# Low parts of two weight chunks per step by ScalarE and an accumulating DMA, in the MLPs of a two-layer hybrid decoder trunk

## The chip, the core and the metric

One NeuronCore of a Trainium2 chip runs the whole program. The metric is the device time of one execution in microseconds (us). Three runs of the kernel before gave 2110.32, 2111.22 and 2113.54 us; the median is 2111.22 us.

## The reference, cut to what matters

Everything is float32: 256 tokens, model width 2048, two layers. Each layer is a mixer and a squared-ReLU MLP with sandwich RMSNorm, and the MLPs are what the change touches:

```python
def sq_relu_mlp(u, w_up, w_down):
    return jnp.square(jax.nn.relu(u @ w_up)) @ w_down

for i in range(DEPTH):                       # DEPTH = 2
    u = rmsnorm(h, mix_pre_g[i])
    m = short_conv_mixer(...) if i == 0 else stick_breaking_mixer(...)
    h = h + rmsnorm(m, mix_post_g[i])
    u = rmsnorm(h, mlp_pre_g[i])
    h = h + rmsnorm(sq_relu_mlp(u, mlp_w_up[i], mlp_w_down[i]), mlp_post_g[i])
```

`w_up` is 2048 x 8192 and `w_down` 8192 x 2048 in each layer.

## The kernel before

**Two parts of every number.** TensorE multiplies in fp32r. Each weight is split into a high part, its fp32r rounding, and a low part, the weight minus the high part. A product is then three matmuls: high by high, high by low, low by high.

**Chunks.** All weights come in one stream of chunks of 128 x 1024 floats (512 KB). `load_one` (L148) issues a chunk's load on SyncE's queue (L157) into one of 5 `raw` buffers. `high_parts` (L167) writes the high part into one of 7 `hi` tiles on ScalarE (L173), and `low_part` writes the low part into one of 7 `lo` tiles on VectorE, as `raw - hi` (L184). A raw buffer is free for a later load when its last reader has finished. The next chunk's load is issued in stream order: SyncE waits at the first load whose buffer is not free, and all later loads wait behind it. The program splits chunks up to four ahead of their use (`chunk`, L239), but a hi or lo tile can be written only when TensorE has read what it held seven tiles earlier.

**An MLP.** Each MLP first computes one eighth of the hidden layer alone (`lead_up`), then runs eight steps `e` = 0 to 7. Steps 0 to 6 have 32 chunks in two halves of 16. A half alternates four times: two chunks of `w_up` for one tile of the next eighth (`whole_up`: 16 high matmuls, L1013, then 16 low ones, L1020), then two chunks of `w_down` for the present eighth (L1120 to L1122). So chunks 0, 1, 4, 5, 8, 9, 12 and 13 of a step belong to `w_up` in the first half; 2, 3, 6, 7 and so on are `w_down`. Most `w_down` pairs take Strassen-Winograd's seven products: `split_seven` makes four differences of the two raw chunks on VectorE (L210) and splits them in four pieces a, b, t, u (L218 on ScalarE, L184 on VectorE), which take four hi and four lo tiles for two chunks.

**What else VectorE and ScalarE do there.** When the up tile is done, ScalarE copies half of its bank out (`half`, L1026), VectorE adds the other half (`s`, L966), ScalarE takes ReLU and square (L967, L968), and both split the result (`hid`). All up tiles of the steps use one PSUM bank, so the next up tile cannot begin before L966 has read the last one.

**GpSimd.** It computes nothing here. Its queue issues accumulating DMAs (L1030, 128 x 512 floats, 256 KB, `mg<-more`) that add the extra products of the seven into the results, nine in each step; they are issued in the second half of a step.

**What sets the order.** TensorE's order is the program's; VectorE's and ScalarE's order in the MLP steps is set by the scheduler when the kernel is built, and so is the choice of the free buffer that a tile takes.

Of the kernel before, what the change touches and what calls it, by code (L numbers as in the profile page):

```python
# [9 lines left out]
F32 = mybir.dt.float32  # L10
F32R = mybir.dt.float32r
AF = mybir.ActivationFunctionType
ALU = mybir.AluOpType
# [33 lines left out]
STEPS = 8  # L47
# [48 lines left out]
def trunk(ctx, tc, x, xT, vecs, rows, ws, out):  # L96
    nc = tc.nc
# [45 lines left out]
    raw, parts, early = {}, {}, {}  # L143
    last_load = [None]
    count = {"loaded": 0, "split": 0, "limit": 1 << 30, "apart": False}
    lows = []
    sevens = {}

    def load_one():
        i = count["loaded"]  # L150
        if i >= len(stream):
            return
        w, c = stream[i]
        t = wpool.tile([P, CW], F32, tag="raw", name=f"raw{i}")
        n = HALF if i < FIRST else CW
        for a in range(0, CW, n):
            last_load[0] = nc.sync.dma_start(t[:, a : a + n], w.ap[c, :, a : a + n])  # L157
        raw[i] = t
        count["loaded"] += 1

    def pieces_of(i):
        w, c = stream[i]
        gains = w.gains(c) if w.gains else [None] * (4 if i < FIRST else 1)
        n = CW // len(gains)
        return [(slice(j * n, (j + 1) * n), gain) for j, gain in enumerate(gains)]

    def high_parts(i):  # L167
        while count["loaded"] <= i:
            load_one()
        hi = wsplit.tile([P, CW], F32R, tag="hi", name=f"whi{i}")  # L170
        lo = wsplit.tile([P, CW], F32R, tag="lo", name=f"wlo{i}")
        for j, (at, gain) in enumerate(pieces_of(i)):
            rounded = nc.scalar.activation(  # L173
                hi[:, at], raw[i][:, at], AF.Copy, scale=1.0 if gain is None else gain
            )
            if j < 2:
                early[i] = rounded
            if not count["apart"]:
                low_part(hi, lo, raw[i], at, gain)
        parts[i] = hi, lo  # L180

    def low_part(hi, lo, t, at, gain):
        if gain is None:
            nc.vector.tensor_tensor(lo[:, at], t[:, at], hi[:, at].bitcast(F32), op=ALU.subtract)  # L184
        else:
            nc.vector.scalar_tensor_tensor(  # L186
                lo[:, at], t[:, at], gain, hi[:, at].bitcast(F32), op0=ALU.mult, op1=ALU.subtract
            )
# [37 lines left out]
    def split_one():  # L226
        i = count["split"]
        if i in sevens:
            split_seven(i)
            return  # L230
        high_parts(i)
        count["split"] += 1
        if count["apart"]:
            lows.append(i)
        else:
            raw.pop(i)
            load_one()
# [138 lines left out]
    h = [None] * NB  # L376
# [310 lines left out]
    W = {"in": Weights(ws["in"]), "out": Weights(ws["out"])}  # L687
# [251 lines left out]
    def mlp(pool, i, before, after):  # L939
# [3 lines left out]
        scale = [None] * NB  # L943
# [89 lines left out]
        def lead_up(to):  # L1033
            first = W["mlp", i, 0].base
            place = {kn: m for m, kn in enumerate(UP_FIRST)}
            lead = list(range(LEAD_UP))
            alone = [(k, n) for k in range(ALONE) for n in lead]
            for b in range(NB):
                for k, n in sorted(alone, key=lambda kn: (kn[0] // 4, kn[1] // 3 if kn[0] < 4 else 0)):
                    high(first, place[k, n], k, n, n + 2, b)  # L1040
            for k, n in alone:
                low(first, place[k, n], k, n)
            for k in range(ALONE, KD):
                for n in lead:
                    high(first, place[k, n], k, n, n + 2)
                for n in lead:
                    low(first, place[k, n], k, n)
                    if k == KD - 1:
                        finish(to, n)
            for n in range(LEAD_UP, NF):  # L1050
                whole_up(to, n, first + 2 * n, (n + 2) % 8)
# [114 lines left out]
        for e in range(STEPS):  # L1166
            for h in range(2):
                for m in SEVEN[e][h]:
                    n = 16 * h + 4 * ORDER[h].index(m) + 2 if e < STEPS - 1 else 8 * h + 2 * m
                    sevens[W["mlp", i, e + 1].base + n] = pool  # L1170
        now = Hidden(0)
        lead_up(now)
        for e in range(STEPS):
# [33 lines left out]
    run(project(W["out"], y, 2, sublayer(mix0)), leave=mix0)  # L1207
    kv = KeyNorms(pool0, None)
    mlp(pool0, 0, mix0, kv)


# [169 lines left out]
    for j in range(4):  # L1381
        for i, (name, to, scale) in enumerate((
            ("k", kT, lambda b: kv.hs[b][:]), ("q", qT, lambda b: held["rq", b][:]),
        )):
            n = 2 * j + i
# [7 lines left out]

    pool1, mix1 = held["pool1"], held["mix1"]
    mlp(pool1, 1, mix1, OutNorms(pool1, None))
    pool1.release()

# [79 lines left out]
```

## Time and profile before

| | |
|---|---|
| median of three runs | 2111.22 us |
| the profiled execution's own time | 2110.45 us |
| its span, first to last instruction | 2108.7 us (1.75 us lie around it) |
| TensorE, weight loads, VectorE, ScalarE, GpSimd busy | 99%, 85%, 87%, 68%, 5% of the span |
| the steps 0 to 6, first and second MLP | about 405 to 990 us, and 1472 to 2057 us |
| granted TensorE clock | 0.999 |

A row of the timeline has the start, the length, the engine, the line and operation, and the tiles written and read (buffer numbers left out). Behind it, in brackets, stands the idle time of the engine before it and what ended it. In the rows of a source line, "us min/median/max" of a DMA is from issue to landing.

### The profile page before, as it was taken

What the parts mean: (1) busy time and instruction counts of PE and PEld (TensorE: products, weight loads), DVE (VectorE), ACT (ScalarE), POOL (GpSimd) and SP (SyncE); (2) the same over time, 40 slices, a digit from 0 to 9 for tenths busy, and PEclk for the clock granted to TensorE, in tenths of its full rate; (3) what the DMA queues carried; (4) which work ended last, traced back from release to release, by engine and by line L of the source; (5) the groups of instructions that cost most, each with busy time, mean ns of one, the idle gap of its engine ahead of it and who ended that gap; (6) DMA issues with size and microseconds to landing.
All of it is one profiled execution on the core that took longest, in us unless ns stands there. A gap on an engine that the chain in (4) does not pass through costs nothing.

```text
span 2108.7 us, 29835 instructions
## 1 busy us (share of the span) xinstructions
PE 2090.4 (99%) x10608; PEld 1782.2 (85%) x10608; DVE 1835.2 (87%) x2807; ACT 1435.2 (68%) x2210; POOL 113.7 (5%) x137
## 2 busy tenths in 40 slices
PE   9999999999999999999999999999999999999998
PEld 8888888888888888888888888889888888888886
DVE  9999965999899999999866777558989999999997
ACT  8656544776776776767567888547767767677674
POOL 0000000010110110101000000000101001011010
PEclk9999999999999999999999999999999999999999
DMA  8467574586777867868575555655778688687683
GB/s 290 155 205 250 191 259 142 190 244 213 232 230 223 265 194 236 250 205 268 173 222 165 160 160 166 218 175 170 199 237 238 213 239 242 210 255 215 220 267 137
DMA packets 132342, 449.23 MB, mean 213 GB/s; under 512 B 14816, under 2 KB 15072, under 8 KB 131168
## 3 DMA queue, kind: packets, MB, share of 16 engines
q1 hardware_dynamic: 113184, 406.55, 58.7%
q0 software_dynamic: 18720, 40.38, 9.9%
q8 instruction: 83, 1.36, 0.3%
q14 instruction: 67, 0.55, 0.1%
q10 hardware_dynamic: 288, 0.39, 0.1%
HBM read 413.19 MB, written 2.10 MB: 197 GB/s over the span
## 4 chain that ended last, share of the span: by engine, by line
PE 91%; DVE 6%; DMA 2%; issue 1%; ACT 1%; DVEq 0%; ACTq 0%
PE up L1013 20%; PE up L1020 11%; PE acc L326 8%; PE acc L328 8%; PE acc L327 8%; PE acc L748 5%; PE more L1121 4%; PE more L1120 4%; PE more L1122 4%; PE acc L1120 4%; PE acc L1121 4%; PE acc L1122 4%; PE lead L748 2%; DVE wlo L184 1%; DMA raw<-w_mlp 1%; PE up L1015 1%
## 5 line engine op out<-in xcount | busy, mean ns | idle before, releaser
L184 DVE TENSOR_TENSOR wlo<-raw,whi 128x1024 fp32r<-128x1024 f32 (+1 forms) x442 | 528.1, 1206 | 87.0 <-ACT whi L173 86.6
L173 ACT ACTIVATE whi<-raw 128x1024 fp32r<-128x1024 f32 (+1 forms) x442 | 453.0, 1043 | 171.1 <-PE acc L328 82.5
L1013 PE MATMUL up<-u,whi 128*128 128x512 f32 x1952 | 465.6, 390 | 3.5 <-DVE s L966 3.5
L1013 PEld LDWEIGHTS up<-u,whi 128*128 128x128 f32 x1952 | 364.6, 188 | 79.9 <-DVE s L966 5.4
L1020 PEld LDWEIGHTS up<-u,wlo 128*128 128x128 f32 x2048 | 263.6, 191 | 10.3
L1020 PE MATMUL up<-u,wlo 128*128 128x256 f32 x2048 | 268.0, 283 | 0.0
L1030 POOL DMA_DIRECT2D mg<-more x108 | 101.7, 1051 | 1280.5 <-ACT s L968 648.3
L186 DVE SCALAR_TENSOR_TENSOR wlo<-raw,gv,whi 128x512 fp32r<-128x512 f32 (+1 forms) x160 | 131.9, 854 | 41.5 <-ACT whi L173 40.8
L210 DVE TENSOR_TENSOR sums<-raw,sums 128x512 f32<-128x512 f32 x236 | 162.1, 687 | 1.3
L173 ACT ACTIVATE whi<-raw,gv 128x512 fp32r<-128x512 f32 (+1 forms) x160 | 121.6, 800 | 48.5 <-PE acc L328 41.8
L326 PE MATMUL acc<-whi,u 128*128 128x512 f32 x384 | 153.1, 399 | 0.1
L328 PE MATMUL acc<-whi,u 128*128 128x512 f32 x384 | 150.0, 391 | 0.0
L327 PE MATMUL acc<-wlo,u 128*128 128x512 f32 x384 | 149.8, 390 | 0.0
L1026 ACT ACTIVATE half<-up 128x256 f32<-128x256 f32 x128 | 48.5, 381 | 89.1 <-PE up L1020 85.5
L748 PE MATMUL acc<-u,whi 128*128 128x512 f32 x416 | 98.9, 391 | 2.7 <-DVE sum L757 2.7
L210 DVE TENSOR_TENSOR sums<-raw,raw 128x512 f32<-128x512 f32 x118 | 81.0, 687 | 23.2 <-DMA raw<-w_mlp 23.0
L967 ACT ACTIVATE s<-s 128x256 f32<-128x256 f32 x128 | 52.4, 413 | 66.3 <-DVE s L966 65.9
L748 PEld LDWEIGHTS acc<-u,whi 128*128 128x128 f32 x416 | 77.4, 188 | 20.5 <-DVE sum L757 3.7
L210 DVE TENSOR_TENSOR sums<-raw 128x512 f32<-128x512 f32 x118 | 81.0, 686 | 11.9 <-DMA raw<-w_mlp 11.7
L328 PEld LDWEIGHTS acc<-whi,u 128*128 128x128 f32 x384 | 72.1, 188 | 15.6
L326 PEld LDWEIGHTS acc<-whi,u 128*128 128x128 f32 x384 | 72.2, 188 | 13.8 <-ACT tk L1309 0.6
L327 PEld LDWEIGHTS acc<-wlo,u 128*128 128x128 f32 x384 | 72.3, 188 | 13.4
(5995 smaller groups left out, 4513.4 us busy)
## 6 DMA issues: line engine op xcount, KB each, us to landing
raw<-w_mlp SPq DMA_DIRECT2D x512, 512.0 KB, 4.6
raw<-w_in SPq DMA_DIRECT2D x94, 512.0 KB, 4.4
mg<-more POOLq DMA_DIRECT2D x108, 256.0 KB, 8.3
raw<-w_out SPq DMA_DIRECT2D x32, 512.0 KB, 4.5
raw<-w_v SPq DMA_DIRECT2D x32, 512.0 KB, 4.3
raw<-w_k SPq DMA_DIRECT2D x32, 512.0 KB, 4.4
raw<-w_q SPq DMA_DIRECT2D x32, 512.0 KB, 4.2
raw<-w_wo SPq DMA_DIRECT2D x32, 512.0 KB, 3.7
```

Source lines behind the costliest of these rows:

```text
L173: rounded = nc.scalar.activation(hi[:, at], raw[i][:, at], AF.Copy, scale=1.0 if gain is None else gain)
L184: nc.vector.tensor_tensor(lo[:, at], t[:, at], hi[:, at].bitcast(F32), op=ALU.subtract)
L210: nc.vector.tensor_tensor(t, x, y, op=ALU.subtract)
L326: nc.tensor.matmul(ps[:], xh, hi[:, a], start=i == 0 and k == 0, stop=False)
L327: nc.tensor.matmul(ps[:], xh, lo[:, a], start=False, stop=False)
L328: nc.tensor.matmul(ps[:], xl, hi[:, a], start=False, stop=i == self.n - 1 and k == self.ks - 1)
L748: nc.tensor.matmul(ps[:, :cols], w, xs[:, :cols], start=k == 0 and part == parts[0], stop=k == KD - 1 and part == parts[1], skip_group_che ...
L1013: nc.tensor.matmul(ps, weight(0, first, m), x, start=k == 0, stop=False)
L1020: nc.tensor.matmul(pss[n][:, :T], weight(1, first, m), x, start=False, stop=k == KD - 1)
L1120: nc.tensor.matmul(self.ps[key][:], xh, hi, start=first, stop=False)
L1121: nc.tensor.matmul(self.ps[key][:], xh, lo, start=False, stop=False)
L1122: nc.tensor.matmul(self.ps[key][:], xl, hi, start=False, stop=last)
```

## The change

```diff
@@ trunk
+    subtracted = set()
@@ high_parts
-            if not count["apart"]:
+            if i in subtracted:
+                nc.scalar.activation(lo[:, at], raw[i][:, at], AF.Copy, scale=-1.0)
+                nc.gpsimd.dma_start(lo[:, at].bitcast(F32), raw[i][:, at], accum_op=ALU.add)
+            elif not count["apart"]:
                 low_part(hi, lo, raw[i], at, gain)
@@ mlp
                     sevens[W["mlp", i, e + 1].base + n] = pool
+                if h == 0 and e < STEPS - 1:
+                    subtracted.update(W["mlp", i, e + 1].base + n for n in (5, 13))
```

For chunks 5 and 13 of steps 0 to 6 of both MLPs, 28 chunks, VectorE's subtraction is replaced. ScalarE writes the raw chunk, rounded as the high part is and negated, into the lo tile, and a DMA on GpSimd's queue adds the raw chunk to it. TensorE now waits for that DMA before the low matmuls of the chunk, and the load that takes the raw buffer next waits for it too. The four new lines move the lines below them: L173 is L174, L184 is L188, L210 is L214, L218 is L222, and those from L966 on are 4 higher.

TensorE's and SyncE's instructions keep their order. On the other engines, step 4 of the first MLP shows the usual place (chunk 13 is `raw_7698` before and `raw_7707` after; `wlo_7798` before and `wlo_7807` after are its lo tile). VectorE before, from the lo part of chunk 12 on:

```order
L184 TENSOR_TENSOR wlo_7784<-raw_7684,whi_7783 128x1024
L210 TENSOR_TENSOR sums<-raw_7757 128x512
L210 TENSOR_TENSOR sums<-raw_7759,raw_7757 128x512
L210 TENSOR_TENSOR sums<-raw_7759,sums 128x512 x2
L184 TENSOR_TENSOR wlo_7798<-raw_7698,whi_7797 128x1024
L966 TENSOR_TENSOR s<-up,half 128x256
L184 TENSOR_TENSOR wlo286a<-raw_7757,whi286a 128x512
```

VectorE after:

```order
L188 TENSOR_TENSOR wlo_7793<-raw_7693,whi_7792 128x1024
L214 TENSOR_TENSOR sums<-raw_7766 128x512
L214 TENSOR_TENSOR sums<-raw_7768,raw_7766 128x512
L214 TENSOR_TENSOR sums<-raw_7768,sums 128x512 x2
L188 TENSOR_TENSOR wlo286a<-raw_7766,whi286a 128x512
L970 TENSOR_TENSOR s<-up,half 128x256
```

The subtraction of chunk 13 is gone, and piece a of the next pair stands ahead of `s`. ScalarE after, at the same place:

```order
L174 ACTIVATE whi_7792<-raw_7693 128x1024
L174 ACTIVATE whi_7806<-raw_7707 128x1024
L222 ACTIVATE whi286a<-raw_7766 128x512
L180 ACTIVATE wlo_7807<-raw_7707 128x1024
L1030 ACTIVATE half<-up 128x256
```

The negated copy (L180) stands between piece a of the next pair and `half`; before, the other four rows followed each other in this order.

In step 0 VectorE's order moves more. Before, behind the lo part of chunk 17 (`wlo_4499`):

```order
L184 TENSOR_TENSOR wlo_4499<-raw_4403,whi_4498 128x1024
L210 TENSOR_TENSOR sums<-raw_4458 128x512
L966 TENSOR_TENSOR s<-up,half 128x256
L210 TENSOR_TENSOR sums<-raw_4460,raw_4458 128x512
L210 TENSOR_TENSOR sums<-raw_4460,sums 128x512
```

After:

```order
L214 TENSOR_TENSOR sums<-raw_4460 128x512
L214 TENSOR_TENSOR sums<-raw_4462,raw_4460 128x512
L214 TENSOR_TENSOR sums<-raw_4462,sums 128x512 x2
L188 TENSOR_TENSOR wlo_4501<-raw_4405,whi_4500 128x1024
L970 TENSOR_TENSOR s<-up,half 128x256
```

Here `s` moves behind three sums and a lo part.

On SyncE the loads keep their order, but one of them waits for the accumulating DMA. Chunks 16 to 21 of step 4 after, with their waits (DMASW is a DMA of GpSimd's queue, DMAHW one of SyncE's):

```order
L158 DMA raw_7796<-w_mlp 128x1024 [waits DMAHW6_49,DVE_49]
L158 DMA raw_7811<-w_mlp 128x1024 [waits DMAHW7_49,DVE_49]
L158 DMA raw_7866<-w_mlp 128x1024 [waits DMAHW1_49,DVE_49]
L158 DMA raw_7868<-w_mlp 128x1024 [waits DMAHW2_49,DVE_49]
L158 DMA raw_7896<-w_mlp 128x1024 [waits DMAHW0_49,DMASW7_49]
L158 DMA raw_7910<-w_mlp 128x1024 [waits DMAHW3_49,DVE_49]
```

The buffer of chunk 13 goes to the load of chunk 20, seven chunks on. So it is, seven on, for 20 of the 28; for chunk 5 of steps 0, 1, 3 and 5 it is the load of chunk 10, five on. In steps 1, 3 and 5 the negated copy of chunk 5 also stands ahead of its high part on ScalarE.

## The prediction

> **What bounds the kernel now.** I read the page first: busy time by engine, the chain that ended last, the two groups of the change.
>
> ```profile
> PE 2090.4 (99%) x10608; PEld 1782.2 (85%) x10608; DVE 1835.2 (87%) x2807; ACT 1435.2 (68%) x2210; POOL 113.7 (5%) x137
> ...
> PE 91%; DVE 6%; DMA 2%; issue 1%; ACT 1%; DVEq 0%; ACTq 0%
> ...
> L184 DVE TENSOR_TENSOR wlo<-raw,whi 128x1024 fp32r<-128x1024 f32 (+1 forms) x442 | 528.1, 1206 | 87.0 <-ACT whi L173 86.6
> L173 ACT ACTIVATE whi<-raw 128x1024 fp32r<-128x1024 f32 (+1 forms) x442 | 453.0, 1043 | 171.1 <-PE acc L328 82.5
> ```
>
> TensorE is the bound: busy 99% of the span and 91% of the chain. VectorE (87%) is second. A lighter VectorE can only return what TensorE waits for it. The waits of TensorE for `s`, and the two places of the four that lie at the ends of step 0:
>
> ```profile
> PE up L1013 <- DVE s L966: 3.5, 4, 1.8
> ```
>
> ```profile
> 478.61 0.50 PE L1013 MATMUL up<-u,whi 128*128 128x512 f32 x1 [0.62 <-DVE s L966]
> ```
>
> ```profile
> 1546.52 0.50 PE L1013 MATMUL up<-u,whi 128*128 128x512 f32 x1 [1.78 <-DVE s L966]
> ```
>
> In both MLPs together TensorE waits 3.5 us, in four places. That is the most that the change can give back (0.17% of 2110.45), and 2.4 us of it (0.62 and 1.78) stand at the ends of step 0. Then the step itself, by the windows view: the first half of step 4.
>
> ```profile
> core 0: us, PE busy (x) PEld busy (x) DVE busy (x) ACT busy (x) POOL busy (x), PEclk, DMA share, GB/s
> 741.00:782.10 41.10, 41.10 (x212) 35.28 (x212) 39.90 (x56) 29.08 (x44) 0.87 (x1) 1.00 0.60 192
> ```
>
> TensorE has no gap here, VectorE is full to 39.9 of 41.1 us without delaying anyone, ScalarE has 12 us free, GpSimd is empty and the DMA engines are 60% busy.
>
> **What is removed and added.** Off VectorE go 28 operations of 1.22 us, 34 us in all; on ScalarE come 28 of about 1.05 (34 and 29 us by the two rows of the page, whose means hold shorter forms too). Neither sum is time of the span: what counts is where each ends beside TensorE. GpSimd gets 28 issues, in halves in which it has nothing queued but the last addition of a step. So nobody waits behind them until the next additions.
>
> **The usual place: chunk 13 of step 4**, on VectorE, ScalarE and TensorE (a merged row of 16 low matmuls is chunk 12's eight, then chunk 13's).
>
> ```profile
> 766.78 1.22 DVE L184 TENSOR_TENSOR wlo<-raw,whi 128x1024 fp32r<-128x1024 f32 x1
> ...
> 774.83 0.69 DVE L210 TENSOR_TENSOR sums<-raw,raw 128x512 f32<-128x512 f32 x1
> ...
> 778.50 0.42 DVE L966 TENSOR_TENSOR s<-up,half 128x256 f32<-128x256 f32 x1
> ```
>
> ```profile
> 763.50 1.06 ACT L173 ACTIVATE whi<-raw 128x1024 fp32r<-128x1024 f32 x1 [0.66 <-PE up L1013]
> 765.32 0.63 ACT L218 ACTIVATE whi286a<-raw 128x512 fp32r<-128x512 f32 x1 [0.75 <-PE up L1013]
> 767.23 0.38 ACT L1026 ACTIVATE half<-up 128x256 f32<-128x256 f32 x1 [1.28 <-PE up L1020]
> ```
>
> ```profile
> 765.12 2.08 PE L1020 MATMUL up<-u,wlo 128*128 128x256 f32 x16
> ...
> 775.44 2.08 PE L1020 MATMUL up<-u,wlo 128*128 128x256 f32 x16
> ...
> 782.14 3.79 PE L1013 MATMUL up<-u,whi 128*128 128x512 f32 x16
> ```
>
> The high part ends at 764.56. The copy stands behind `whi286a`, which ends at 765.95, and needs a lo tile. Seven tiles back is chunk 8's, read by the first eight matmuls of the row at 765.12; with 0.12 us between starts they end at about 766.25. So the copy runs from 766.3 to 767.35, in the gap of 1.28 us before `half`, which comes 0.1 us late. Behind the copy wait only `half` and, through it, `s`, which has until 782.14 minus 778.92, that is 3.2 us, to spare one tile later. **The cost on ScalarE is nothing.** Without that gap it would be up to 1.05 us of lateness, still within the 3.2.
>
> The DMA must land before the ninth matmul of the row at 775.44, at 776.4. Its price is not in the trace at 512 KB. The nearest rows are the 256 KB additions: all 108, the one that found the DMA engines freest, and ScalarE's operation that released that one.
>
> ```profile
> L1030 POOL DMA_DIRECT2D mg<-more x108: 860/872/1922, 449.9 to 2032.1; - x108
> ...
> DMA to landing us min/median/max: 3.3/8.3/12.3
> ```
>
> ```profile
> L1030 POOL DMA_DIRECT2D mg<-more x1: 869/869/869, 533.5 to 533.5; - x1
> ...
> DMA to landing us min/median/max: 3.3/3.3/3.3
> ```
>
> ```profile
> 532.62 0.60 ACT L1082 ACTIVATE more<-more 128x512 f32<-128x512 f32 x1
> ```
>
> ```profile
> q1 hardware_dynamic: 113184, 406.55, 58.7%
> q0 software_dynamic: 18720, 40.38, 9.9%
> ```
>
> ScalarE ended at 533.22, GpSimd began at 533.51: 0.29 us between them. GpSimd's queue takes 9.9% of 2108.7 us for 40.38 MB, 5.2 us for a MB, so the second 256 KB cost 1.4 us: an estimate of **4.7 us** alone. A load on SyncE's queue costs 3.0 us for a MB, 1.6 for a chunk. Two loads are issued near the DMA; one ahead of it makes 6.3, both make 7.9. The row's median, with 1.4 more, gives 9.7, its maximum 13.7; but those additions run in trains of nine, and GpSimd's queue is empty here. I take **6.3**, nearest to the fastest row; 4.7 and 13.7 stay as ends. The copy's end plus 0.29 is 767.64: landing at 773.9, **2.5 us before it is needed**. The limit is 8.8 us.
>
> [...]
>
> **The tight place: chunk 5 of step 0**, on ScalarE and TensorE.
>
> ```profile
> 410.13 1.06 ACT L173 ACTIVATE whi<-raw 128x1024 fp32r<-128x1024 f32 x1
> 411.08 0.42 ACT L968 ACTIVATE s<-s 128x256 f32<-128x256 f32 x1
> ```
>
> ```profile
> 419.41 2.08 PE L1020 MATMUL up<-u,wlo 128*128 128x256 f32 x16
> ```
>
> The copy follows the square, from 411.4 to 412.5; the DMA is issued at 412.75 and needed at 419.41 + 0.96 = 420.4. The limit is 7.6 us: 1.3 to spare with 6.3, short by 0.3 with 7.9. There are four such places, two in each MLP's step 0; I count nothing for them.
>
> **The raw buffers.** Chunk 13's was free at 768.0, the end of VectorE's row; now at 773.9. The load that takes it is chunk 20's: before, issue, landing, and ScalarE's use.
>
> ```profile
> L157 SPq DMA_DIRECT2D raw<-w_mlp x1: 327/327/327, 770.3 to 770.3; - x1
> ...
> DMA to landing us min/median/max: 4.8/4.8/4.8
> ```
>
> ```profile
> 784.14 1.07 ACT L173 ACTIVATE whi<-raw 128x1024 fp32r<-128x1024 f32 x1
> ```
>
> It now lands at 773.9 + 4.8 = 778.7, 5.4 us before its use, and holds up SyncE's queue by 3.6 us at most. Nothing. If that cover went, what is late next is VectorE's sums and behind them `s`, with its 3.2 us.
>
> **What comes back.** In step 0 of the first MLP the chain of waits leaves TensorE at 441 and is VectorE's until a load that ends late:
>
> ```profile
> 440.23 0.90 PE up L1020 x8
> 441.12 0.21 DVE wlo L184
> ...
> 457.60 10.08 DMA raw<-w_mlp
> ```
>
> Two subtractions (2.4 us) less stand ahead of that, but at the same place `s` moves behind three sums and a lo part. The return lies between 0 and the 2.4 us of both ends; I take two thirds, 1.6, since the load is issued as soon as VectorE frees its buffer. The other 1.1 of the 3.5 us stand at the end of step 1, where no chain leads back to the first half.
>
> **Sum**: 2110.45 - 1.6 + 0 + 0 = 2108.85 us against the profiled execution. The median is 0.77 above that execution, so the forecast is **2109.6 us**.
>
> **The rivals.**
> 1. *The low part comes late* (slower). The accumulating DMA becomes TensorE's wait, from 8.8 us on at usual places, 7.6 in step 0. For it: the median addition takes 8.3 at half the size, and loads run beside. Against it: the queue is empty. At 9.7 us: 18 usual places (12 of chunk 13, 6 of chunk 5 in even steps) of 0.9, four of 2.1, 25 us: **2136**. The 6 of chunk 5 in steps 1, 3 and 5 have their copy earlier.
> 2. *The load is held* (slower). In 8 places (chunk 5 of steps 0, 1, 3, 5) the load five chunks on waits for the DMA, and VectorE's in-order sums behind it, then `s`. It decides where the load comes over 3.2 us late; at 4.2 late, 8 us: **2119**. Against it: only 8 places, and the DMA alone needs 4.7.
> 3. *VectorE's relief returns whole*: all 3.5 us, **2107.7**; against it, two of the four waits lie a step away.
> 4. *The change moves nothing*: the relief is lost behind the reordered `s`, **2111.2**.
>
> **How the numbers follow.** Forecast 0.40 (2108 to 2111), rival 4 0.12, rival 3 0.10, rival 1 0.27, rival 2 0.11. The range runs from 2106.3, a little under rival 3, to 2130, which leaves out the worse half of rival 1. About 0.2% (4.2 us) is what a measurement of this kernel can tell from no change. Faster by more would need more than all 3.5 us: 0.08. Slower by more has rival 1 but for its lightest cases and two thirds of rival 2: 0.32. Within: 0.60.
>
> **What would show it.** Right: the DMA of L181 lands in 5 to 8 us, no wait of L1024 (the low matmuls) on it, the waits for `s` under 3.5 us. Wrong: idle time of L1024 in each first half (rival 1); VectorE idle before L214 on a load and TensorE before L1017 on `s` (rival 2). A landing over 8.8 us overturns the forecast.

## The result and the profile after

The changed kernel takes 2124.0 us (median of 13 runs, 2113.22 to 2127.11), the kernel before 2110.77 (13 runs, 2107.91 to 2113.54): a ratio of 1.0053, 95% interval 1.0039 to 1.0067, or 8 to 14 us slower. The forecast was 2109.6 us and no change that can be measured; the time lies within the range, but the sign is the other one. The profiled execution is one of the longer ones, 2126.41 us with a span of 2124.7.

The page after, the lines that answer to those of before (busy time, DMA queues, chain, groups):

```profile
PE 2099.1 (99%) x10608; PEld 1785.9 (84%) x10608; DVE 1807.6 (85%) x2779; ACT 1455.2 (68%) x2238; POOL 138.0 (6%) x165
...
q0 software_dynamic: 22752, 55.06, 14.1%
...
PE 86%; DVE 8%; DMA 4%; issue 1%; ACT 1%; SPq 0%; DVEq 0%; ACTq 0%
...
L1017 PE MATMUL up<-u,whi 128*128 128x512 f32 x1952 | 471.6, 393 | 9.7 <-DVE s L970 9.5
...
L214 DVE TENSOR_TENSOR sums<-raw,raw 128x512 f32<-128x512 f32 x118 | 80.8, 685 | 40.5 <-DMA raw<-w_mlp 40.3
...
L214 DVE TENSOR_TENSOR sums<-raw 128x512 f32<-128x512 f32 x118 | 80.7, 684 | 28.4 <-DMA raw<-w_mlp 28.3
```

VectorE has less work, as was meant (its lo parts L184, now L188, take 493.3 us in place of 528.1; in all it is busy 28 us less), and TensorE waits more for it: 9.5 us for `s` where it was 3.5. VectorE itself waits for weight loads: 68.6 us ahead of its sums (40.3 and 28.3), before 34.7 (23.0 and 11.7). In the chain VectorE has 8% and the DMAs 4%, up from 6% and 2%. The new DMAs, all 28:

```profile
L181 POOL DMA_DIRECT2D wlo<-raw x28: 869/869/904, 415.3 to 2017.4; - x28
...
DMA to landing us min/median/max: 5.2/6.2/8.1
```

They land in 6.2 us (forecast 6.3), and no low matmul (L1024) waits for one. So the loss is not where the prediction looked for it.

TensorE's program is the same in both kernels, so its 10608 matmuls can be laid beside each other one by one. The lag of the changed kernel grows to 16.0 us in few places:

| place (its waits and half pace, less the later waits of before that go) | lag, us |
|---|---|
| up to 400 us, where every engine's program is still the same | 2.8 |
| end of step 0, first MLP (chunk 24) | 3.2 |
| end of step 6, first MLP (chunk 24) | 3.7 |
| end of step 0, second MLP (chunk 24) | 3.4 |
| all the rest | 2.9 |

The first row is chance; it was 0.2 to 3.4 in the profiles of the other runs. The three in the middle look alike. TensorE's timeline after, at these three places; the second row is the same block of 16 matmuls at a place without a wait:

```profile
472.71 5.54 PE L1017 MATMUL up<-u,whi 128*128 128x512 f32 x16 [2.31 <-DVE s L970]
...
1534.89 3.79 PE L1017 MATMUL up<-u,whi 128*128 128x512 f32 x16
...
977.96 5.51 PE L1017 MATMUL up<-u,whi 128*128 128x512 f32 x16 [1.83 <-DVE s L970]
...
1548.99 3.35 PE L1017 MATMUL up<-u,whi 128*128 128x512 f32 x7 [3.61 <-DVE s L970]
```

Each place is a wait of 1.8 to 3.6 us for `s`, and then a block that takes 5.5 us in place of 3.8: seven or eight of its matmuls start 0.43 us apart in place of 0.23. The windows view has the granted clock (PEclk) beside it, two stretches of 10 us, one around such a wait and one behind another:

```profile
core 0: us, PE busy (x) PEld busy (x) DVE busy (x) ACT busy (x) POOL busy (x), PEclk, DMA share, GB/s
...
470.00:480.00 10.00, 7.69 (x35) 6.15 (x33) 10.00 (x17) 7.10 (x11) 0.00 (x0) 0.83 0.78 236
...
980.00:990.00 10.00, 10.00 (x48) 8.49 (x47) 9.96 (x13) 7.43 (x12) 0.55 (x1) 0.88 0.92 337
```

So each of these three waits is paid twice: 1.8 to 3.6 us itself, and 1.4 to 1.6 us at half pace behind it.

Why `s` is late in step 0 is seen on VectorE. After, then before, at the end of step 0 of the first MLP:

```profile
467.02 0.69 DVE L214 TENSOR_TENSOR sums<-raw 128x512 f32<-128x512 f32 x1 [3.09 <-DMA raw<-w_mlp]
469.90 0.69 DVE L214 TENSOR_TENSOR sums<-raw,raw 128x512 f32<-128x512 f32 x1 [2.19 <-DMA raw<-w_mlp]
470.50 1.22 DVE L188 TENSOR_TENSOR wlo<-raw,whi 128x1024 fp32r<-128x1024 f32 x1
471.64 0.68 DVE L214 TENSOR_TENSOR sums<-raw,sums 128x512 f32<-128x512 f32 x1
472.24 0.41 DVE L970 TENSOR_TENSOR s<-up,half 128x256 f32<-128x256 f32 x1
```

```profile
465.17 0.69 DVE L210 TENSOR_TENSOR sums<-raw 128x512 f32<-128x512 f32 x1 [2.65 <-DMA raw<-w_mlp]
465.78 1.22 DVE L184 TENSOR_TENSOR wlo<-raw,whi 128x1024 fp32r<-128x1024 f32 x1
466.91 0.42 DVE L966 TENSOR_TENSOR s<-up,half 128x256 f32<-128x256 f32 x1
467.70 0.69 DVE L210 TENSOR_TENSOR sums<-raw,raw 128x512 f32<-128x512 f32 x1 [0.37 <-DMA raw<-w_mlp]
```

The sum that reads two raw chunks needs chunk 27, whose load takes 10 us here in both kernels (10.9 after, 10.1 before), beside the train of additions (seven `mg<-more` in steps 0 and 1, eight in each later one, not the nine named above). Before, `s` stood ahead of it; now it stands behind it, the low part of chunk 25 and one more sum. This is a second reordering of step 0, two tiles behind the one that the prediction names. Two theories then: **A**, the order of VectorE in step 0 makes the loss; **B**, the DMAs make the loads late, whatever the order.

### The profile page after: what moved, and what is told of

Its sections match the earlier page's. It is cut to its first block, busy times and chain, and to the rows that moved or that the text cites. A ratio compares the mean times of both kernels' runs of the same rounds, so it can differ in the third digit from the quotient of the medians.

```text
span 2124.7 us, 29897 instructions
## 1 busy us (share of the span) xinstructions
PE 2099.1 (99%) x10608; PEld 1785.9 (84%) x10608; DVE 1807.6 (85%) x2779; ACT 1455.2 (68%) x2238; POOL 138.0 (6%) x165
## 4 chain that ended last, share of the span: by engine, by line
PE 86%; DVE 8%; DMA 4%; issue 1%; ACT 1%; SPq 0%; DVEq 0%; ACTq 0%
PE up L1017 19%; PE up L1024 10%; PE acc L330 7%; PE acc L332 7%; PE acc L331 7%; PE more L1125 4%; PE more L1124 4%; PE more L1126 4%; PE acc L752 4%; PE acc L1124 4%; PE acc L1125 4%; PE acc L1126 4%; DMA raw<-w_mlp 3%; DVE wlo L188 2%; DVE sums L214 1%; PE lead L752 1%
## 5 line engine op out<-in xcount | busy, mean ns | idle before, releaser
L188 DVE TENSOR_TENSOR wlo<-raw,whi 128x1024 fp32r<-128x1024 f32 (+1 forms) x414 | 493.3, 1202 | 88.2 <-ACT whi L174 87.4
L174 ACT ACTIVATE whi<-raw 128x1024 fp32r<-128x1024 f32 (+1 forms) x442 | 452.3, 1042 | 161.7 <-PE acc L332 81.9
L1017 PE MATMUL up<-u,whi 128*128 128x512 f32 x1952 | 471.6, 393 | 9.7 <-DVE s L970 9.5
L1024 PEld LDWEIGHTS up<-u,wlo 128*128 128x128 f32 x2048 | 263.6, 191 | 10.3
L1024 PE MATMUL up<-u,wlo 128*128 128x256 f32 x2048 | 268.0, 283 | 0.0
L214 DVE TENSOR_TENSOR sums<-raw,sums 128x512 f32<-128x512 f32 x236 | 161.4, 684 | 1.8
L174 ACT ACTIVATE whi<-raw,gv 128x512 fp32r<-128x512 f32 (+1 forms) x160 | 121.6, 800 | 48.4 <-PE acc L332 41.9
L214 DVE TENSOR_TENSOR sums<-raw,raw 128x512 f32<-128x512 f32 x118 | 80.8, 685 | 40.5 <-DMA raw<-w_mlp 40.3
L214 DVE TENSOR_TENSOR sums<-raw 128x512 f32<-128x512 f32 x118 | 80.7, 684 | 28.4 <-DMA raw<-w_mlp 28.3
L181 POOL DMA_DIRECT2D wlo<-raw x28 | 24.5, 874 | 930.8 <-ACT half L1030 735.1
```

Source lines behind the costliest of these rows:

```text
L174: rounded = nc.scalar.activation(hi[:, at], raw[i][:, at], AF.Copy, scale=1.0 if gain is None else gain)
L214: nc.vector.tensor_tensor(t, x, y, op=ALU.subtract)
L1017: nc.tensor.matmul(ps, weight(0, first, m), x, start=k == 0, stop=False)
L1024: nc.tensor.matmul(pss[n][:, :T], weight(1, first, m), x, start=False, stop=k == KD - 1)
```

## The experiments

All against runs of the kernel before that were taken together with them; "in us" is the ratio's interval times 2111.

| run | median us | ratio [95%] | in us | TensorE waits for `s` | VectorE's sums wait for loads |
|---|---|---|---|---|---|
| the change | 2124.0 | 1.0053 [1.0039, 1.0067] | 8 to 14 | 9.5 | 68.6 |
| the change again | 2121.24 | 1.0043 [1.0029, 1.0057] | 6 to 12 | 11.2 | 66.0 |
| e1_order | 2113.17 | 1.0012 [1.0002, 1.0021] | 0 to 4 | 4.7 | 56.7 |
| e2_steps1to6 | 2115.34 | 1.0018 [1.0009, 1.0027] | 2 to 6 | 6.4 | 58.5 |
| e4_nodma | 2112.21 | 1.0006 [0.9997, 1.0015] | -1 to 3 | 2.8 | 44.4 |
| b_late | 2112.34 | 1.0006 [0.9997, 1.0014] | -1 to 3 | 4.8 | 33.2 |
| b_exact | 2118.55 | 1.0033 [1.0023, 1.0043] | 5 to 9 | 6.0 | 34.2 |
| e5_fromhi | 2120.26 | 1.0040 [1.0027, 1.0053] | 6 to 11 | 5.7 | 57.1 |
| e6_plain | 2112.69 | 1.0008 [0.9999, 1.0017] | 0 to 4 | 4.3 | 41.2 |
| e7_only13 | 2124.87 | 1.0063 [1.0050, 1.0076] | 11 to 16 | 10.4 | 58.2 |
| e8_only5 | 2115.54 | 1.0022 [1.0010, 1.0034] | 2 to 7 | 2.5 | 42.5 |
| a_trains | 2108.81 | 0.9988 [0.9979, 0.9996] | -4 to -1 | 1.1 | 45.0 |
| b_trains | 2108.75 | 0.9988 [0.9979, 0.9997] | -4 to -1 | 0.4 | 14.9 |
| a_trains_nodma | 2107.54 | 0.9980 [0.9971, 0.9989] | -6 to -2 | none | 16.4 |

The last two columns are of one profile each, the medians of 5 to 13 runs. The profiles of b_exact, e8_only5 and b_trains are of the fastest of their runs, those of a_again, e2_steps1to6 and b_late of the slowest.

**The order alone mended (e1_order).** Edges without a semaphore put two sums behind `s` at the end of step 0 of both MLPs; all else is the change (NOSYNC is the kind of the edge).

```
             made = nc.vector.tensor_tensor(t, x, y, op=ALU.subtract)
+            if t is t3 or t is t2:
+                waits_for.setdefault(i, []).append(made)
...
+                    if e == 0 and h == 1 and n == 2:
+                        for made in waits_for[at_chunk + 2]:
+                            tc.add_manual_dep(made.ins, last_s[0].ins.name, NOSYNC, reason="s first")
                     whole_up(new, 4 * h + n, at_chunk, UP_BANK)
```

> The change, with one edit to VectorE's order in step 0 of both MLPs: where the third seven of the second half is split (chunks 26 and 27), the two sums that read chunk 27 are queued behind the s of the tile before, as in the kernel before. Theory A (in step 0 the change put s behind sums that wait for a late load; TensorE then waits over 2 us and runs eight more matmuls at half its pace): the places in the trace of the changed kernel are worth 3.2 + 3.4 = 6.6 us, so 2124.0 - 6.6 = 2117 us, and no TensorE wait over 2 us in step 0. Theory B (the added DMAs, or the raw buffers that they hold, make the loads late, whatever the order): 2122 to 2124 us.

2113.17 us: all but 2 us of the loss are gone, more than A said. VectorE at the end of step 0 of the first MLP:

```profile
466.43 0.69 DVE L215 TENSOR_TENSOR sums<-raw 128x512 f32<-128x512 f32 x1 [1.85 <-DMA raw<-w_mlp]
...
468.77 0.42 DVE L973 TENSOR_TENSOR s<-up,half 128x256 f32<-128x256 f32 x1
469.10 0.68 DVE L215 TENSOR_TENSOR sums<-raw,raw 128x512 f32<-128x512 f32 x1
```

`s` is ready at 469.2, and TensorE, whose next block starts at 470.80, does not wait. The end of step 6 costs less here too (a wait of 1.18 us and full pace behind it), which the edit does not touch; why is not settled. In the other profiles of the change and of its parts with accumulating DMAs in step 6 and this order there, that wait is between nothing and 1.94 us.

**Without step 0 (e2_steps1to6).** 
```
-                if h == 0 and e < STEPS - 1:
+                if h == 0 and 0 < e < STEPS - 1:
                     subtracted.update(W["mlp", i, e + 1].base + n for n in (5, 13))
```

> The change in steps 1 to 6 only (24 chunks); step 0 as before. Theory A: the 6.6 us of step 0 are gone, 2117 us. Theory B: the loss goes by the number of DMAs, 24/28 of 13.2 us stay, 2122 us.

2115.34 us. Two thirds of the loss hang on step 0's four chunks, more than A said, and B's 2122 by the number of DMAs is out. This run takes the order and the DMAs of step 0 away together, so it cannot part the two.

**Without the DMAs (e4_nodma).** 
```
                 nc.scalar.activation(lo[:, at], raw[i][:, at], AF.Copy, scale=-1.0)
-                nc.gpsimd.dma_start(lo[:, at].bitcast(F32), raw[i][:, at], accum_op=ALU.add)
```

> The change without the accumulating DMAs: ScalarE writes the negated high part, VectorE does nothing, and the raw chunk is not added, so that the low products of 28 chunks are computed from other numbers; the raw buffer is free from ScalarE's copy on. VectorE's and ScalarE's orders are those of the changed kernel. Theory A: the order alone costs, 2117 to 2124 us, and the waits for s of step 0 stay. Theory B: without DMAs the loads are early again, 2107 to 2111 us.

2112.21 us: with the bad order in place, hardly anything is lost. That fits B. TensorE waits 0.9 and 1.1 us at the two ends of step 0, with full pace behind it.

**The order alone on the kernel before (b_late).** The edge of e1_order the other way round, for the sum `t2` alone:

```
+                        for made in waits_for[at_chunk + 2]:
+                            tc.add_manual_dep(last_s[0].ins, made.ins.name, NOSYNC, reason="s behind")
```

> The kernel before, with the order of step 0 alone: in both MLPs the s ahead of the third seven of the second half is queued behind the two sums that read chunk 27. No ScalarE copies, no DMAs. Theory A: in the trace of before these sums end at 469.0 and 1536.9 us where TensorE is ready at 467.5 and 1534.5; with s behind them it waits about 2.3 and 3.2 us, with some 1.5 us at half pace behind each, less the later waits of 0.6 and 1.8 that go: 2110.8 + 6 = 2115 to 2118 us. Theory B: 2110.8 us.

2112.34 us, which again seems to speak against A. But the scheduler put the low part of chunk 25 ahead of the sums here, so that `s` came 1.2 us earlier than in the changed kernel. The waits were 1.1 and, in the second MLP's timeline of TensorE, this:

```profile
1540.18 3.92 PE L1016 MATMUL up<-u,whi 128*128 128x512 f32 x16 [2.58 <-DVE s L969]
```

**The exact order on the kernel before (b_exact).** Edges for the very sequence of the changed kernel: the sum of two chunks (`t3`), the low part of chunk 25, one sum (`t2`), `s`.

```
+                        t3_made, t2_made = waits_for[at_chunk + 2]
+                        for later, ahead in ((made_low[at_chunk + 1], t3_made), (t2_made, made_low[at_chunk + 1]), (last_s[0], t2_made)):
+                            tc.add_manual_dep(later.ins, ahead.ins.name, NOSYNC, reason="order")
```

> The kernel before, with VectorE's order at the end of step 0 of both MLPs exactly as in the changed kernel: the sum that waits for chunk 27, the low part of chunk 25, one more sum, then s. No ScalarE copies, no DMAs. Against the milder order (2112.3 us, waits of 1.2 and 2.7 us) s comes 1.2 us later at each place. If the order is enough for the loss of step 0: waits of 2.4 and 3.9 us, half pace of 1.5 us behind each, less 2.4 us of later waits that go, 2110.9 + 7 = 2117 to 2118 us. If the DMAs are needed: 2112 to 2114 us.

2118.55 us: without any DMA or copy, the order alone costs 5 to 9 us, as A's 6.6 said for step 0. In its profiled run, the fastest at 2114.03 us, the two waits are 1.92 and 2.99 us with full pace behind them; what the 4.5 us more of the median run are is in no profile. The second of the two:

```profile
1539.92 1.42 PE L1016 MATMUL up<-u,whi 128*128 128x512 f32 x5 [2.99 <-DVE s L969]
```

So A is right for the order, and e4_nodma shows that something in the change can pay for it.

**The same again (a_again).** No edit.

> The changed kernel once more, beside the others of this call, for a second profile. If the loss sits in few places where TensorE waits over 2 us for s and then runs eight matmuls at half pace (step 0 of both MLPs, end of step 6 of the first), these show again, and the time is 2121 to 2127 us in most runs, near 2113 us in a run in which no wait passes 2 us. If the places are chance, they show elsewhere.

2121.24 us. The same three places, and the end of step 6 of the second MLP as a fourth, which the first profile does not have; TensorE's timeline at three of them:

```profile
470.71 5.52 PE L1017 MATMUL up<-u,whi 128*128 128x512 f32 x16 [2.93 <-DVE s L970]
...
975.35 5.52 PE L1017 MATMUL up<-u,whi 128*128 128x512 f32 x16 [1.94 <-DVE s L970]
...
2050.34 3.96 PE L1017 MATMUL up<-u,whi 128*128 128x512 f32 x10 [3.32 <-DVE s L970]
```

The end of step 0 of the second MLP has a wait of 2.50 us and half pace too. The three places are the kernel's, not chance.

**What the DMAs do: hold or traffic (e5_fromhi).** 
```
-                nc.gpsimd.dma_start(lo[:, at].bitcast(F32), raw[i][:, at], accum_op=ALU.add)
+                nc.gpsimd.dma_start(lo[:, at].bitcast(F32), hi[:, at].bitcast(F32), accum_op=ALU.add)
```

> The change with the 28 DMAs reading the high part's tile in place of the raw chunk: the same bytes at the same moments, but the raw buffer is free from ScalarE's copy on. It adds the high part to its own negative, so the low part of these chunks is left out (zero). VectorE's and ScalarE's orders are those of the changed kernel. Theory C (the raw buffer held for 6 us more makes the loads late): as without the DMAs, 2111 to 2114 us. Theory D (the DMAs' traffic makes the loads late): as the change, 2121 to 2125 us.

2120.26 us beside 2121.24 for the change, just under D's range and far from C's. The raw buffer that is held longer is worth nothing that shows: it is the traffic (theory D). Two things differ besides. These DMAs land in 7.0 to 9.4 us, and here the low matmuls wait for them, 1.5 us in three places. And in e4_nodma and e5_fromhi, by what releases the loads, the raw buffers come round to them in another turn than in the changed kernel: in step 0 of the second MLP the load of chunk 18 waits for piece a of the pair before (`wlo542a`) in the changed kernel and the load of chunk 19 does in these two, where chunk 18's is issued about 2 us earlier. Between these two runs VectorE's and ScalarE's orders are the same and the DMAs differ, and that is worth some 8 us. The place to look at is the load of chunk 19 in step 0 of the second MLP, which runs beside the DMA of chunk 13. Its rows by line, in the changed kernel (the middle one is who waited for it):

```profile
L158 SPq DMA_DIRECT2D raw<-w_mlp x1: 519/519/519, 1513.5 to 1513.5; - x1
...
  DVE sums L214: 2.4, 1
...
DMA to landing us min/median/max: 7.3/7.3/7.3
```

Without the DMAs (e4_nodma):

```profile
L158 SPq DMA_DIRECT2D raw<-w_mlp x1: 328/328/328, 1503.2 to 1503.2; - x1
...
DMA to landing us min/median/max: 3.7/3.7/3.7
```

With DMAs that only copy (e6_plain, below):

```profile
L158 SPq DMA_DIRECT2D raw<-w_mlp x1: 328/328/328, 1507.0 to 1507.0; - x1
...
  DVE sums L214: 1.4, 1
...
DMA to landing us min/median/max: 5.8/5.8/5.8
```

7.3 us against 3.7 (7.5 in e5_fromhi, 3.7 before), and VectorE waits 2.4 us for it. In the other profiles with an accumulating DMA beside this load it took 5.6 to 6.5 us, and 3.5 to 4.8 with no DMA of GpSimd's beside it.

From there the lateness runs on. With each time counted from when TensorE is ready for the next up tile at the end of the step, the load of chunk 22, which waits for VectorE, is issued at -21.3 us in the changed kernel, at -23.3 without the DMAs; chunk 27's load lands at +0.8 against -1.8, and TensorE waits 3.6 us for the `s` behind it against 1.1. In both, `s` is done 2.8 us after that landing; so it is in b_exact, where the load lands at +0.1 and TensorE waits 3.0. Before, it landed at +1.4. Taken from these profiles, VectorE's relief brings the load 3 us forward and the DMAs push it 2.6 us back. The sizes are not firm: without copies and DMAs it also landed at +0.9, +0.1 and -0.8 (b_late, b_exact, b_trains), and with the relief alone at -0.4 (a_trains_nodma).

**Copying in place of accumulating (e6_plain).** 
```
-                nc.gpsimd.dma_start(lo[:, at].bitcast(F32), raw[i][:, at], accum_op=ALU.add)
+                nc.gpsimd.dma_start(lo[:, at].bitcast(F32), raw[i][:, at])
```

> The change with the 28 DMAs copying instead of accumulating: the same tiles, bytes and orders of all engines, but the raw chunk replaces the negated high part, so the low products of these chunks are computed from other numbers. From the page an added accumulating DMA takes 3.2 us of each of the 16 DMA engines (14.1% of 2124.7 us less 9.9% of 2108.7, over 28), a plain load of the same size 1.6. Theory D (the DMA engines' time that the loads lose): half the lateness, so at the end of step 0 waits under 2 us without half pace behind them, 2112 to 2117 us. Theory E (a DMA of GpSimd's at that place, whatever its work): 2121 us as before.

2112.69 us, at the lower end of D's range, and E is out: with the same orders, what is lost hangs on the accumulation. From the page's queue line these DMAs take 12.0% of 2112.5 us, 1.6 us of the 16 engines each; the accumulating ones 3.2. The load of chunk 19 alone does not part the two: its 5.8 us beside a copy lie among the 5.6 to 7.5 beside an accumulation.

**Which of the two chunks (e7_only13, e8_only5).** The first of the two; the second has `(5,)`:

```
-                    subtracted.update(W["mlp", i, e + 1].base + n for n in (5, 13))
+                    subtracted.update(W["mlp", i, e + 1].base + n for n in (13,))
```

> The change for chunk 13 alone (14 DMAs); s stays behind the late sums in step 0, as in the changed kernel. If the chain begins at the load of chunk 19, which runs beside the DMA of chunk 13 (7.3 us in place of 3.7 us in step 0 of the second MLP): most of the loss stays, 2117 to 2122 us. If it goes by the number of DMAs: half, 2116 us.

> The change for chunk 5 alone (14 DMAs); s stays behind the late sums in step 0. By the chain from chunk 19's load: little, as the kernel without any of the DMAs, 2111 to 2114 us. By the number of DMAs: 2116 us.

Chunk 13 alone loses as much as both, 2124.87 us, so the loss does not go by the number of DMAs. But the forecast's chain is not what its trace shows: here chunk 13's buffer goes to the load of chunk 19 itself, which waits 4.75 us for the DMA in step 0 of the second MLP, is issued 4.4 us later than in the changed kernel (-27.4 against -31.8 us) and then takes 3.7 us. In this run it is the held buffer that makes this load late, as in rival 2, and VectorE has half the relief, so that it is no clean test of the traffic. Chunk 5 alone is between the two forecasts, 2115.54 with runs from 2111 to 2123; it does not tell them apart.

**`s` ahead in every step (a_trains, b_trains).** The edit of e1_order with one condition less, on the change and on the kernel before:

```
-                    if e == 0 and h == 1 and n == 2:
+                    if h == 1 and n == 2:
```

> The change, with s ahead of the sums that read chunk 27 at that place in every step that has a seven there, not in step 0 alone. If what remained with step 0 mended (2113.2 us, waits of 1.0 to 1.9 us at four such places of other steps) is the same mechanism, those waits go: 2109 to 2111 us. If it is something else, 2113 us as before.

> The kernel before with the same edit of the order in every step, no ScalarE copies, no DMAs. Of the 3.5 us of waits for s in the trace of before, those behind a late chunk 27 go, at most 1 us in each MLP, since the wait at the end of step 0 has VectorE busy ahead of it: 2108 to 2111 us.

Both are faster than either kernel, 2108.81 and 2108.75 us. So the waits of the other steps were the same mechanism but for 1.1 us that stay in a_trains. In the second, b_trains, the waits of TensorE for `s` are all but gone:

```profile
PE up L1016 <- DVE s L969: 0.4, 1, 0.4
```

**The same without the DMAs (a_trains_nodma).** a_trains with the line of L181 taken out.

> The change with s ahead in every step and without the accumulating DMAs, so that the raw chunk is not added and the low products of 28 chunks are computed from other numbers. VectorE's and ScalarE's orders are those of the run with s ahead in every step (2108.8 us, 1.1 us of waits for s). If the DMAs still cost something there that VectorE's relief pays: 2107 to 2108 us. If neither is worth anything once s stands ahead: 2108.5 to 2109 us.

2107.54 us and no wait for `s`. The intervals of the three overlap: VectorE's relief may be worth 1 to 2 us, and the DMAs take as much.

## Why the prediction was wrong

- **The DMA's price, the copy's and the issue's: right in themselves.** Landing 5.2/6.2/8.1 us against 6.3, no wait of the low matmuls on it, GpSimd idle ahead of each of the 28, ScalarE's copy without effect (e4_nodma keeps it: -1 to 3 us). Rival 1 does not occur in the changed kernel.
- **The first step that failed: contention was counted one way only, and the DMAs' effect on the loads was put at nothing.** The working let a load make the DMA late ("one ahead of it makes 6.3") and never let the DMA make the load late; "nobody waits behind them" looked at GpSimd's queue and not at the 16 engines. The page had the price: 5.2 us of the engines for a MB of accumulation against 3.0 for a load. The load of chunk 19 paid it, 7.3 us in place of 3.7, and accumulating in place of copying made the difference between 2112.69 us (e6_plain) and 2121 to 2124.
- **"The raw buffers": nothing, and for the changed kernel nothing shows.** At the usual place, step 4, chunk 20's load was issued 5.2 us later against TensorE, more than the 3.6 allowed for, and still landed 3.0 us before the next up tile. Rival 2 had the symptoms (VectorE idle on a load, TensorE on `s`) and nearly the size; its mechanism, the held buffer, is not needed for the loss (e5_fromhi). It does occur with chunk 13 alone (e7_only13).
- **The second step that failed: the bound of "What comes back".** It set the return between 0 and 2.4 us with `s` moved behind three sums, and saw only the reordering of chunk 18's tile. At chunk 26's the `s` went behind a sum that waits for a load of 10 us. The lower end should have been a loss: from before's own rows that sum ends at 468.4, and with the low part, one sum and `s` itself behind it `s` is done at about 470.5 where TensorE is ready at 467.5. b_exact shows that this alone is 5 to 9 us, where the sum counted a gain of 1.6.
- **What no part of the prediction had is the half pace** behind the waits of 2.31, 1.83 and 3.61 us, 1.4 to 1.6 us at each of the three places.
- **That the time lies within the range is luck.** The range was drawn up to 2130 us for rivals 1 and 2, and neither is what made the loss.

Put together: the order costs 5 to 9 us (b_exact), with the change's copies and VectorE's relief but no DMAs nearly all of it is paid back (e4_nodma), by earlier loads as far as the profiles show, and the accumulating DMAs take that back and add step 6 (the change), where `s` stands behind the same sums in the kernel before too. With `s` ahead neither matters much (a_trains, b_trains). Open are how much of the payment is VectorE's relief and how much the other turn of the raw buffers in e4_nodma, how the held buffer and the halved relief add up to the loss with chunk 13 alone, and why the end of step 6 was mild in e1_order.

## What to carry to other kernels

Price a transfer not only by when it lands but by the DMA-engine time that it takes from the loads beside it, and look which of those loads has no slack; a transfer that no matmul waits for can still make the end later (the changed kernel loses 8 to 14 us, without its 28 DMAs -1 to 3). Where a scheduler sets an engine's order, list what the change puts ahead of each operation that the bounding engine waits for, and price it by the load that it may wait for, with loss as one end. Here pinning one order, with no change of the work, was worth more than the change (b_trains, 1 to 4 us faster).

## What the runs showed of the hardware

- **TensorE at half pace after a wait.** Taken as the time lost between the starts of two matmuls (0.16 us more than the idle time in the rows), no wait for `s` up to 1.96 us was followed by it in the 15 profiles; of the 13 from 1.99 to 3.77 us ten were, for 7 to 12 matmuls 0.43 us apart, 3 to 5 us in all; 2.08 and 3.15 us (b_exact) and 2.74 us (b_late) were not. The shortest that was, 1.99 us, is the row with 1.83 us at the end of step 6 of the changed kernel. What decides it at one length or another, no run shows.
- **An accumulating DMA took twice the engine time of a copy** of the same tiles: 3.2 us of the 16 engines for 512 KB (2.7 in e5_fromhi, where it read the high part's tile) against 1.6 (e6_plain), landing in 6.2 against 4.0 us at the median, 5.2 against 3.1 at the fastest.
